# Hybrid encoder layer on one core: the last products in two banks, the final norms in another order, the first two tiles shared by ScalarE and DVE

## The chip, the cores and the metric

The kernel runs on one core of a Trainium2 chip. The metric is the device time of one execution in microseconds, taken as the median of several runs.

## The reference

One encoder layer in float32 on x of 512 positions and 1024 channels, and a final RMSNorm. Cut to what matters:

```python
def rms_norm(x, g):
    y = x * lax.rsqrt(jnp.mean(x * x, axis=-1, keepdims=True) + EPS)
    return y * g
...
h = rms_norm(x, attn_norm_g)
xr, gate, q, k, v = split(h @ w_in)          # 1024 -> 5 x 512
xr = centred_depthwise_conv(xr, conv_w, conv_b)
y_rnn = (rg_lru(xr, forward) + rg_lru(xr, backward)) * gelu(gate)
y_attn = dilated_attention(q, k, v, rel_bias)  # 8 heads, three dilated windows
mix = concat(rms_norm(y_rnn, norm_rnn_g), rms_norm(y_attn, norm_attn_g))
x = x + mix @ w_out                            # 1024 -> 1024
h = rms_norm(x, mlp_norm_g)
x = x + square(relu(h @ w_up)) @ w_down        # 1024 -> 4096 -> 1024
return rms_norm(x, final_norm_g)
```

## The kernel before

Every product of the projections is made of three matrix products in a reduced-precision float32 format ("fp32r"): each operand is split into a rounded part (hi) and the rest (lo = value - hi), and hi x hi, hi x lo and lo x hi are added in a PSUM bank. In the helper `mm3` these three are lines 303, 304 and 305. ScalarE mostly makes the hi part (a copy with rounding, line 251 for the weights), DVE the lo part (a subtraction, line 259). The order of the instructions on TensorE, ScalarE, DVE and GpSimd is the order in which the program writes them; only SP's queue of transfers is ordered by the framework.

**The start.** x comes transposed, in 8 tiles of 128 channels by 512 positions, each with 128 x 384 weights beside it (`xwt[k]`, lines 315 to 327). For each tile `cvx(k)` makes `h_hi` (x times the norm's gain, rounded, ScalarE, line 333), the weights' hi part (line 336 on DVE for tile 0, line 338 on ScalarE for the others), `h_lo` (line 339, DVE) and the weights' lo part `w3l` (line 340, DVE). `sq(k)` squares the tile on ScalarE, `addsq(k)` adds the squares into `sqx` on DVE (line 348). TensorE first runs 8 warm-up products (line 145). Then it works through the tiles in order, for three blocks of 128 output columns in three banks (`pxr`): tile 0 with the three blocks inside (line 412), the other tiles with `mm3` for one block after the other. Ahead of tile 7's products stands `col_sums(sqx)` (line 402), which sums the squares over the channels for the norm's factor; `rstd_cols` makes that factor on GpSimd. `softplus_consts` is a generator that makes eight-column constants for the recurrence on DVE, ScalarE and GpSimd in four portions; `next(spc)` issues a portion. Two are issued ahead of and behind tile 0, a third behind its square, the fourth much later.

**The middle** (input projection, recurrence, attention, output projection, and the MLP in two halves, with products of quadrants that share operands) is not touched.

**The end.** The down projection of the MLP's second half works through seven groups of products, of which "s4" is the last. It has two row tiles (`tt` 0 and 1), each with 4 x 2 steps of three products of 512 columns that are added onto a bank in which earlier groups stand already. The row tiles belong to positions 256 to 383 and 384 to 511, that is to the blocks 2 and 3 of the output; blocks 0 and 1 are complete after the group before. `x1n[g, n]` holds block g, column half n of the residual stream. `fin_half` squares a half and sums it over the row (ScalarE, line 1301). `fin(g)` adds the sums of both halves (line 1306), takes the root (line 1307, ScalarE) and the reciprocal (line 1308, DVE), multiplies the right half on ScalarE (line 1310; `xf` is that half times the gain already, line 1340) and issues its output from ScalarE's queue (line 1311), and multiplies the left half with factor and gain on DVE (line 1313) and issues it from SP's queue. `fin_other(g)` prepares the right half of block g. While the first row tile of "s4" runs, the norms of blocks 0 and 1 and `fin_other` of blocks 2 and 3 are issued; behind it come the addition `evac` (line 1488) and the norm of block 2, and behind the second row tile `fin_last`, which adds the product to the left half of the output (512 columns, worked on in two pieces of 256: lines 1319 and 1321), squares the pieces (lines 1320 and 1322), and makes root, reciprocal (1325, 1326) and outputs (1328 to 1333).

Of the kernel before, what the change touches and what calls it, by code (L numbers as in the profile page):

```python
# [14 lines left out]
AF = mybir.ActivationFunctionType  # L15
OP = mybir.AluOpType

P = 128
S = 512
D = 1024  # L20
# [13 lines left out]
HF = NF // 2  # L34
NQ = HF // 4
TH = S // 2

VEC = {}
_o = 0
# [60 lines left out]
def hybrid_kernel(ctx: ExitStack, tc, xw, xn, w_in, w_v, w_out, w_up, w_dn, gates, vecs, rel, onehot, fg, out):  # L100
    nc = tc.nc
# [28 lines left out]
    def vec(n, i):  # L130
        return vt[:, VEC[n] + i:VEC[n] + i + 1]
# [41 lines left out]
        yield cneg, chalf  # L173

    spc = softplus_consts()
    next(spc)


    chunks = []
# [122 lines left out]
    def mm3(o, a, b, first, last, on=False):  # L302
        nc.tensor.matmul(o, lhsT=a[0], rhs=b[0], start=bool(first), stop=False, skip_group_check=on)  # L303
        nc.tensor.matmul(o, lhsT=a[0], rhs=b[1], start=False, stop=False, skip_group_check=on)  # L304
        nc.tensor.matmul(o, lhsT=a[1], rhs=b[0], start=False, stop=bool(last), skip_group_check=on)  # L305
# [8 lines left out]
    h_hi = big.tile([P, KD, S], FR, name="h_hi", tag="bigA")  # L314
# [15 lines left out]

    def cvx(k):
        x, w = xwt[k][:, :S], xwt[k][:, S:]
        act(h_hi[:, k, :], x, AF.Copy, scale=vec("ag", k))
        hi, lo = g_("w3h", FR), g_("w3l", FR)
        if k == 0:
            nc.vector.tensor_copy(hi[:, :3 * P], w)
        else:
            act(hi[:, :3 * P], w, AF.Copy)
        stt(h_lo[:, k, :], x, vec("ag", k), f(h_hi)[:, k, :], op0=OP.mult, op1=OP.subtract)
        nc.vector.tensor_tensor(lo[:, :3 * P], w, f(hi)[:, :3 * P], op=OP.subtract)  # L340
        w3.append((hi, lo))

    def sq(k):
        sqx[k] = g_("sqx")
        act(sqx[k], xwt[k][:, :S], AF.Square)
# [2 lines left out]
        nc.vector.tensor_tensor(sqx[0], sqx[0], sqx.pop(k), op=OP.add)  # L348

    cvx(0)  # L350
    next(spc)
    sq(0)
    next(spc)
    for k in range(1, KD):
        cvx(k)
        sq(k)
        if k >= 2:
            addsq(k - 1)
# [532 lines left out]
    x1, x1n = {}, {}  # L891
# [237 lines left out]
    r2 = {}  # L1129
# [168 lines left out]
    def fin_half(tt, n):  # L1298
        s = small("sso", 1)
        scr = g_("scr")  # L1300
        act(scr, x1n[tt, n], AF.Square, accum_out=s)
        sso[tt, n] = s

    def fin(tt):
        r = small("rf", 1)
        nc.vector.tensor_tensor(r, sso[tt, 0], sso[tt, 1], op=OP.add)
        act(r, r, AF.Sqrt, scale=1.0 / D, bias=epsb)
        nc.vector.reciprocal(r, r)
        o = g_("ot")
        act(o, xf[tt], AF.Copy, scale=r)  # L1310
        nc.scalar.dma_start(out[tt * P:(tt + 1) * P, S:], o)
        o = g_("ot")
        stt(o, x1n[tt, 0], r, fgt[0], op0=OP.mult, op1=OP.mult)
        nc.sync.dma_start(out[tt * P:(tt + 1) * P, 0:S], o)

    def fin_last(tt, p):
        x, sa, sb, b = x1n[tt, 0], small("sso", 1), small("sso", 1), small("rf", 1)
        left, right = slice(0, TH), slice(TH, S)
        stt(x[:, left], p[:, left], r2[tt], x[:, left], op0=OP.mult, op1=OP.add)
        act(g_("scr")[:, left], x[:, left], AF.Square, accum_out=sa)  # L1320
        stt(x[:, right], p[:, right], r2[tt], x[:, right], op0=OP.mult, op1=OP.add)
        nc.vector.tensor_tensor_reduce(g_("scr")[:, right], x[:, right], x[:, right], 1.0, 0.0, OP.mult, OP.add, sb)
        act(b, sa, AF.Identity, scale=1.0 / D, bias=sso[tt, 1])
        r = small("rf", 1)
        act(r, sb, AF.Sqrt, scale=1.0 / D, bias=b)
        nc.vector.reciprocal(r, r)
        o = g_("ot")
        act(o, xf[tt], AF.Copy, scale=r)
        nc.scalar.dma_start(out[tt * P:(tt + 1) * P, S:], o)
        o = g_("ot")  # L1330
        for c in (left, right):
            stt(o[:, c], x[:, c], r, fgt[0][:, c], op0=OP.mult, op1=OP.mult)
            nc.sync.dma_start(out[tt * P:(tt + 1) * P, c], o[:, c])
# [23 lines left out]
    for half in range(2):  # L1357
# [132 lines left out]
        def evac(w, tt, p):  # L1490
            if w == "11":
                add(p, 0, tt, 0)
            elif w == "s1":
                add(p, 1, tt, 1)
            elif w == "s2":
                add(p, 0, tt, 1)
            elif w == "22":
                add(p, 0, tt, 1)
            elif w == "s3":
                add(p, 1, tt, 1)  # L1500
            elif w == "21":
                add(p, 0, tt, 0)
            else:
                add(p, 1, tt, 0)
                if half == 1:
                    fin_half(2 + tt, 0)
                    fin(2 + tt)

        def dmm(j, dst, tt, k2):
            _, w, q = seq[j]  # L1510
            hi, lo = splits[cd + j]
            sl = slice(k2 * S, (k2 + 1) * S)
            ah, al = opsplit[w, q]
            tsl = slice(k2 * TH + tt * P, k2 * TH + (tt + 1) * P)
            mm3(dst[tt], (ah[:, tsl], al[:, tsl]), (hi[:, sl], lo[:, sl]), q == 0 and k2 == 0 and w in ("11", "s1", "21"), q == NQ - 1 and k2 == 1, True)

        def dfeed(j, m):
            if m == 0:
                conv_hi(cd + j + 3)
            elif m == 1:  # L1520
                conv_lo(cd + j + 3)
            elif m == 2 and todo:
                a_hi(*todo[0])
            elif m == 3 and todo:
                a_lo(*todo.popleft())
# [36 lines left out]
                    nc.sync.dma_start(fgt[n], bass.AP(tensor=fg.tensor, offset=fg.offset + n * S, ap=[[0, P], [1, S]]))  # L1562
        if half == 1:
            b = 6 * NQ
            for tt in range(2):
                for j in range(b, b + NQ):
                    for k2 in range(2):
                        dmm(j, dst["s4"], tt, k2)
                        if tt == 0:
                            dfeed(j, 2 + k2)  # L1570
                    if tt == 0 and j == b:
                        conv_hi(cd + b + 3)
                        conv_lo(cd + b + 3)
                    if tt == 0 and j in (b + 1, b + 2):
                        fin_half(j - b - 1, 0)
                        fin(j - b - 1)
                    if tt == 0 and j == b + 3:
                        fin_other(2)
                        fin_other(3)
                if tt == 0:  # L1580
                    evac("s4", tt, dst["s4"][tt])
                else:
                    fin_last(3, dst["s4"][1])


# [54 lines left out]
```

## Time and profile before

| | |
|---|---|
| median of 3 runs | 543.67 us (543.66 to 544.35) |
| the profiled execution's own time | 544.4 us |
| its span, first to last instruction | 542.2 us |
| TensorE clock granted, mean | 0.997 |
| busy share: TensorE, weight loads, DVE, ScalarE, GpSimd | 98%, 84%, 80%, 67%, 12% |
| moved by DMA | 106.96 MB, mean 197 GB/s |

The profile is that of one execution. Times in its rows are microseconds from the span's start, and a row of the timeline gives start, length, engine, line, operation, output and inputs, and in brackets how long the engine was idle before it and what ended that. PE is TensorE's products, PEld its weight loads, which overlap the products; DVE is VectorE, ACT is ScalarE, POOL is GpSimd; SPq and ACTq are the queues that issue transfers. In rows of groups, the numbers behind the bar are the busy time in all in microseconds and the mean of one in nanoseconds.

### The profile page before, as it was taken

The numbers are of one execution on the slowest core, as the hardware profiler recorded it, in microseconds if no ns is written. First come the engines' busy times: TensorE is split into PE (matmuls) and PEld (weight loads), VectorE is DVE, ScalarE is ACT, GpSimd is POOL, SyncE is SP. The second block draws the span as 40 slices with busy tenths as digits, with TensorE's granted clock in tenths as the row PEclk, the third lists the DMA queues.
The fourth block names the chain that finished last, engine by engine and source line by source line (L and its number), as shares of the span: only waits on it lengthen the run. The fifth ranks groups of instructions, "written<-read, shape, count | busy, mean of one in ns | idle before, by whom it ended". The sixth has DMA issues, their size and how long they took to land.

```text
span 542.2 us, 8156 instructions
## 1 busy us (share of the span) xinstructions
PE 533.5 (98%) x3018; PEld 452.9 (84%) x3018; DVE 431.6 (80%) x628; ACT 363.4 (67%) x573; POOL 64.1 (12%) x91
## 2 busy tenths in 40 slices
PE   9999999999999999999999999999999999999994
PEld 7856888887887578889999888888999999888883
DVE  6897788996673599889769987879755888886984
ACT  7667983798774755677566855565645777755665
POOL 3330000000001031001030223001001020131000
PEclk9999999999999999999999999999999999999998
DMA  7754276454398788855676799994987397799704
GB/s 273 230 163 142 54 246 182 132 180 143 83 343 215 178 152 204 296 202 160 192 156 167 204 253 273 284 366 104 283 236 205 113 191 199 195 283 262 191 1 157
DMA packets 34360, 106.96 MB, mean 197 GB/s; under 512 B 4228, under 2 KB 5124, under 8 KB 34320
## 3 DMA queue, kind: packets, MB, share of 16 engines
q1 hardware_dynamic: 25600, 76.56, 41.4%
q0 software_dynamic: 7968, 28.76, 28.4%
q10 hardware_dynamic: 752, 1.12, 0.6%
q8 instruction: 24, 0.39, 0.3%
q14 instruction: 16, 0.13, 0.1%
HBM read 98.00 MB, written 4.23 MB: 189 GB/s over the span
## 4 chain that ended last, share of the span: by engine, by line
PE 87%; DVE 4%; ACT 4%; DMA 3%; issue 1%; ACTq 0%; DVEq 0%
PE pd L304 8%; PE pd L303 8%; PE pd L305 8%; PE pu L305 7%; PE pu L303 7%; PE pu L304 7%; PE pqk L303 3%; DMA tw<-in_w_up_dram 3%; PE pwo L303 3%; PE pqk L305 3%; PE pqk L304 3%; PE pav L859 3%; PE pt L778 3%; PE pwo L305 3%; PE pwo L304 3%; DVE wlo L259 2%
## 5 line engine op out<-in xcount | busy, mean ns | idle before, releaser
L259 DVE TENSOR_TENSOR wlo<-wraw,whi 128x1024 fp32r<-128x1024 f32 x73 | 89.0, 1221 | 21.4 <-ACT whi L251 21.1
L251 ACT ACTIVATE whi<-wraw 128x1024 fp32r<-128x1024 f32 x70 | 74.0, 1059 | 34.6 <-PE pd L305 19.5
L303 PE MATMUL pd<-whi,ah 128*128 128x512 f32 x192 | 74.7, 389 | 0.0
L304 PE MATMUL pd<-wlo,ah 128*128 128x512 f32 x192 | 74.7, 389 | 0.0
L305 PE MATMUL pd<-whi,al 128*128 128x512 f32 x192 | 74.7, 389 | 0.0
L251 ACT ACTIVATE whi<-tw 128x1024 fp32r<-128x1024 f32 x36 | 38.0, 1059 | 40.0 <-DMA tw<-in_w_up_dram 13.3
L304 PE MATMUL pu<-hl,whi 128*128 128x256 f32 x224 | 63.4, 283 | 0.0
L305 PE MATMUL pu<-hh,wlo 128*128 128x256 f32 x224 | 63.4, 283 | 0.0
L303 PE MATMUL pu<-hh,whi 128*128 128x256 f32 x224 | 63.4, 283 | 0.0
L305 PE MATMUL pu<-h2h,wlo 128*128 128x256 f32 (+1 forms) x200 | 60.1, 301 | 0.6 <-DVE wlo L259 0.6
L303 PE MATMUL pu<-h2h,whi 128*128 128x256 f32 (+1 forms) x200 | 60.1, 300 | 0.0
L304 PE MATMUL pu<-h2l,whi 128*128 128x256 f32 (+1 forms) x200 | 60.0, 300 | 0.0
L259 DVE TENSOR_TENSOR wlo<-tw,whi 128x1024 fp32r<-128x1024 f32 x36 | 44.0, 1223 | 19.5 <-ACT whi L251 19.5
L303 PEld LDWEIGHTS pu<-hh,whi 128*128 128x128 f32 x224 | 43.0, 192 | 0.0
L304 PEld LDWEIGHTS pu<-hl,whi 128*128 128x128 f32 x224 | 43.0, 192 | 0.0
L305 PEld LDWEIGHTS pu<-hh,wlo 128*128 128x128 f32 x224 | 43.0, 192 | 0.0
L251 ACT ACTIVATE whi<-ts 128x1024 fp32r<-128x1024 f32 x24 | 25.5, 1061 | 25.3 <-PE pd L305 18.3
L303 PEld LDWEIGHTS pd<-whi,ah 128*128 128x128 f32 x192 | 36.0, 188 | 7.5
L305 PEld LDWEIGHTS pd<-whi,al 128*128 128x128 f32 x192 | 36.0, 188 | 7.5
L304 PEld LDWEIGHTS pd<-wlo,ah 128*128 128x128 f32 x192 | 36.0, 188 | 7.4
L305 PEld LDWEIGHTS pu<-h2h,wlo 128*128 128x128 f32 x200 | 38.2, 191 | 2.1 <-DVE wlo L259 0.8
L304 PEld LDWEIGHTS pu<-h2l,whi 128*128 128x128 f32 x200 | 38.3, 191 | 1.3
(261 smaller groups left out, 1262.8 us busy)
## 6 DMA issues: line engine op xcount, KB each, us to landing
wraw<-in_w_up_dram SPq DMA_DIRECT2D x25, 512.0 KB, 4.1
ts<-in_w_dn_dram POOLq DMA_DIRECT2D x24, 512.0 KB, 13.9
wraw<-in_w_dn_dram SPq DMA_DIRECT2D x24, 512.0 KB, 9.2
tw<-in_w_up_dram SPq DMA_DIRECT2D x15, 512.0 KB, 9.9
tw<-in_w_up_dram POOLq DMA_DIRECT2D x15, 512.0 KB, 7.8
wraw<-in_w_in_dram SPq DMA_DIRECT2D x13, 512.0 KB, 3.5
ts<-in_w_dn_dram SPq DMA_DIRECT2D x8, 512.0 KB, 5.0
tw<-in_w_dn_dram SPq DMA_DIRECT2D x8, 512.0 KB, 8.0
```

The source lines that it names most:

```text
L251: act(hi, raws[i], AF.Copy)
L259: nc.vector.tensor_tensor(lo, r, f(splits[i][0]), op=OP.subtract)
L303: nc.tensor.matmul(o, lhsT=a[0], rhs=b[0], start=bool(first), stop=False, skip_group_check=on)
L304: nc.tensor.matmul(o, lhsT=a[0], rhs=b[1], start=False, stop=False, skip_group_check=on)
L305: nc.tensor.matmul(o, lhsT=a[1], rhs=b[0], start=False, stop=bool(last), skip_group_check=on)
L778: nc.tensor.transpose(pt[:, qt * P:(qt + 1) * P], en[h][qt][:, jt * P:(jt + 1) * P], ident)
L859: nc.tensor.matmul(pav[p][a, :], lhsT=vs[:, jt, h * DH:(h + 1) * DH], rhs=et.pop((h, jt)), start=jt == 0, stop=jt == 3)
```

## The change

Five edits, at the start and at the end of the kernel:

- Tiles 0 and 1: `h_hi` is made by ScalarE (256 columns of tile 0, 384 of tile 1) and by DVE (the other columns), and the weights' hi part by DVE for both tiles.
- Tile 1's products run like those of tile 0: hi x hi for the three blocks, then hi x lo, then lo x hi.
- The first three portions of the softplus constants are issued behind `cvx(1)`, `cvx(2)` and `cvx(3)`.
- The final norms are split into `fin_r` (sum and root) and `fin` and stand in another order: `fin_other(2)`, then block 0, block 1's root, `fin_other(3)`, and behind the first row tile block 2's square, block 1's outputs, block 2's root and outputs. All their outputs go through SP's queue.
- The last row tile's products: five of the eight steps with 512 columns as before, the last three (`NL`) for the left 256 columns into the same bank, and then for the right 256 columns into another bank (`pr`). `fin_left` adds the first bank (both halves, the right one without the last three steps) and squares the left piece while the right products run; `fin_right` adds the second bank, squares the right piece and makes the outputs. The gain is multiplied in ahead of the factor, so that the outputs are multiplications by a column: 512 columns on DVE, and of the other half 384 columns on ScalarE and 128 (`AC`) on DVE.

```diff
+NL = 3
+AC = 128
...
     spc = softplus_consts()
-    next(spc)
...
     def cvx(k):
         x, w = xwt[k][:, :S], xwt[k][:, S:]
-        act(h_hi[:, k, :], x, AF.Copy, scale=vec("ag", k))
         hi, lo = g_("w3h", FR), g_("w3l", FR)
-        if k == 0:
+        if k < 2:
+            c = (2 * P, 3 * P)[k]
+            act(h_hi[:, k, :c], x[:, :c], AF.Copy, scale=vec("ag", k))
+            nc.vector.tensor_scalar(h_hi[:, k, c:], x[:, c:], vec("ag", k), None, op0=OP.mult)
             nc.vector.tensor_copy(hi[:, :3 * P], w)
         else:
+            act(h_hi[:, k, :], x, AF.Copy, scale=vec("ag", k))
             act(hi[:, :3 * P], w, AF.Copy)
...
     cvx(0)
-    next(spc)
     sq(0)
-    next(spc)
     for k in range(1, KD):
         cvx(k)
+        if k < 4:
+            next(spc)
         sq(k)
...
-        if k == 0:
+        if k < 2:
             for i, (a, b) in enumerate(((0, 0), (0, 1), (1, 0))):
                 for t in range(3):
-                    nc.tensor.matmul(pxr[t], lhsT=wk(t, 0)[a], rhs=hk(0)[b], start=i == 0, stop=False)
+                    nc.tensor.matmul(pxr[t], lhsT=wk(t, k)[a], rhs=hk(k)[b], start=i == 0 and k == 0, stop=False)
             continue
...
-    def fin(tt):
-        r = small("rf", 1)
+    rfs = {}
+
+    def fin_r(tt):
+        r = rfs[tt] = small("rf", 1)
         nc.vector.tensor_tensor(r, sso[tt, 0], sso[tt, 1], op=OP.add)
         act(r, r, AF.Sqrt, scale=1.0 / D, bias=epsb)
+
+    def fin(tt):
+        r = rfs.pop(tt)
         nc.vector.reciprocal(r, r)
         o = g_("ot")
         act(o, xf[tt], AF.Copy, scale=r)
-        nc.scalar.dma_start(out[tt * P:(tt + 1) * P, S:], o)
+        nc.sync.dma_start(out[tt * P:(tt + 1) * P, S:], o)
...
+    def fin_left(tt, p):
+        x, sa, b = x1n[tt, 0], small("sso", 1), small("rf", 1)
+        xf[tt, 0] = g_("xf")
         stt(x[:, left], p[:, left], r2[tt], x[:, left], op0=OP.mult, op1=OP.add)
         act(g_("scr")[:, left], x[:, left], AF.Square, accum_out=sa)
         stt(x[:, right], p[:, right], r2[tt], x[:, right], op0=OP.mult, op1=OP.add)
+        nc.vector.tensor_tensor(xf[tt, 0][:, left], x[:, left], fgt[0][:, left], op=OP.mult)
+        act(b, sa, AF.Identity, scale=1.0 / D, bias=sso[tt, 1])
+        return b
+
+    def fin_right(tt, p, b):
+        x, sb, r = x1n[tt, 0], small("sso", 1), small("rf", 1)
+        stt(x[:, right], p[:, right], r2[tt], x[:, right], op0=OP.mult, op1=OP.add)
         nc.vector.tensor_tensor_reduce(g_("scr")[:, right], x[:, right], x[:, right], 1.0, 0.0, OP.mult, OP.add, sb)
         act(r, sb, AF.Sqrt, scale=1.0 / D, bias=b)
+        nc.vector.tensor_tensor(xf[tt, 0][:, right], x[:, right], fgt[0][:, right], op=OP.mult)
         nc.vector.reciprocal(r, r)
+        rows = out[tt * P:(tt + 1) * P, :]
+        o, o1 = g_("ot"), g_("ot")
+        act(o1[:, AC:], xf[tt][:, AC:], AF.Copy, scale=r)
+        nc.scalar.dma_start(rows[:, S + AC:], o1[:, AC:])
+        nc.vector.tensor_scalar(o, xf[tt, 0], r, None, op0=OP.mult)
+        nc.sync.dma_start(rows[:, :S], o)
+        nc.vector.tensor_scalar(o1[:, :AC], xf[tt][:, :AC], r, None, op0=OP.mult)
+        nc.sync.dma_start(rows[:, S:S + AC], o1[:, :AC])
...
+                if j == b:
+                    conv_hi(cd + b + 3)
+                    conv_lo(cd + b + 3)
+                    fin_other(2)
+                if j == b + 1:
+                    fin_half(0, 0)
+                    fin_r(0)
+                if j == b + 2:
+                    fin_half(1, 0)
+                    fin(0)
+                    fin_r(1)
+                    fin_other(3)
+            evac("s4", 0, dst["s4"][0])
+            fin_half(2, 0)
+            fin(1)
+            fin_r(2)
+            fin(2)
+            ks = [(j, k2) for j in range(b, b + NQ) for k2 in range(2)]
+            for j, k2 in ks[:-NL]:
+                dmm(j, dst["s4"], 1, k2)
+            for j, k2 in ks[-NL:]:
+                dmm(j, dst["s4"], 1, k2, left)
+            pr = ps_("pd", "pj")
+            for j, k2 in ks[-NL:]:
+                dmm(j, [None, pr], 1, k2, right, (j, k2) == ks[-NL])
+            bl = fin_left(3, dst["s4"][1])
+            fin_right(3, pr, bl)
```

More of the change, by code (lines that the diff above doesn't have):

```diff
@@ L1314, in fin @@
         nc.sync.dma_start(out[tt * P:(tt + 1) * P, 0:S], o)
-    def fin_last(tt, p):
-        x, sa, sb, b = x1n[tt, 0], small("sso", 1), small("sso", 1), small("rf", 1)
-        left, right = slice(0, TH), slice(TH, S)
+    def fin_left(tt, p):
+        x, sa, b = x1n[tt, 0], small("sso", 1), small("rf", 1)
+        xf[tt, 0] = g_("xf")
         stt(x[:, left], p[:, left], r2[tt], x[:, left], op0=OP.mult, op1=OP.add)
@@ L1504, in evac, with dmm @@
                 add(p, 1, tt, 0)
[L1505 to L1509, printed above, removed]
+        def dmm(j, dst, tt, k2, c=slice(0, S), new=False):
             _, w, q = seq[j]
             hi, lo = splits[cd + j]
-            sl = slice(k2 * S, (k2 + 1) * S)
+            sl = slice(k2 * S + c.start, k2 * S + c.stop)
             ah, al = opsplit[w, q]
             tsl = slice(k2 * TH + tt * P, k2 * TH + (tt + 1) * P)
-            mm3(dst[tt], (ah[:, tsl], al[:, tsl]), (hi[:, sl], lo[:, sl]), q == 0 and k2 == 0 and w in ("11", "s1", "21"), q == NQ - 1 and k2 == 1, True)
+            mm3(dst[tt][:, c], (ah[:, tsl], al[:, tsl]), (hi[:, sl], lo[:, sl]), new or q == 0 and k2 == 0 and w in ("11", "s1", "21"), q == NQ - 1 and k2 == 1, True)
         def dfeed(j, m):
@@ L1564, in hybrid_kernel @@
             b = 6 * NQ
[L1565 to L1583, printed above, removed]
+            for j in range(b, b + NQ):
+                for k2 in range(2):
+                    dmm(j, dst["s4"], 0, k2)
+                    dfeed(j, 2 + k2)
+                if j == b:
[25 more added lines that the diff above has]
+            fin_right(3, pr, bl)
 def kernel(**inputs):
```

9 lines of the change are left out of this document (removed).

## The prediction

> **What bounds the kernel now.** I read the page's first part, then its chain, then the chain again as a list in order of time, and last the instructions of the first 21 us and of the last 10 us, because the diff touches only these.
>
> ```profile
> span 542.2 us, 8156 instructions
> PE 533.5 (98%) x3018; PEld 452.9 (84%) x3018; DVE 431.6 (80%) x628; ACT 363.4 (67%) x573; POOL 64.1 (12%) x91
> PE 87%; DVE 4%; ACT 4%; DMA 3%; issue 1%; ACTq 0%; DVEq 0%
> ```
>
> TensorE is busy for 98% of the span and carries 87% of the chain. So time is won only where TensorE waits, or after its last product. The list of waits has one row of TensorE in the middle of the kernel:
>
> ```profile
> PE pu L305 <- DVE wlo L259: 0.6, 1, 0.6
> ```
>
> The change leaves that place alone. The start is in the chain in order of time (start, length, what):
>
> ```profile
> 1.04 3.79 PE pwarm L145 x16
> ...
> 7.79 0.37 PE pxr L303
> 8.16 0.38 PE pxr L304
> 8.54 0.46 PE pxr L305
> ```
>
> The last three are the first products of tile 1 of x; the first row is the warm-up, behind which tile 0 begins. A product that waits for nothing takes 0.227 us (at the end: 534.86 - 529.42 = 5.44 us for 24 of them, rows below). Three would take 0.68 us and took 0.37 + 0.38 + 0.46 = 1.21 us: 0.53 us are lost, because the three need in turn the rounded weights, the rest of x and the rest of the weights of this tile, one operation late each. The operations, by the timeline:
>
> ```profile
> 3.78 0.17 DVE L153 SCALAR_TENSOR_TENSOR e<-vt 128x8 f32<-128x8 f32 x1 [2.78 <-DMA vt<-in_vecs_dram]
> 3.86 0.17 DVE L154 TENSOR_SCALAR sp<-vt 128x8 f32<-128x8 f32 x1
> ...
> 5.67 0.17 DVE L158 TENSOR_SCALAR z<-e 128x8 f32<-128x8 f32 x1
> 5.87 0.20 DVE L159 RECIPROCAL z<-z 128x8 f32<-128x8 f32 x1
> 6.47 0.72 ACT L333 ACTIVATE h_hi<-tw,vt 128x512 fp32r<-128x512 f32 x1 [1.36 <-DMA tw<-in_xw_dram]
> 7.23 0.75 DVE L339 SCALAR_TENSOR_TENSOR h_lo<-tw,vt,h_hi 128x512 fp32r<-128x512 f32 x1 [1.16 <-ACT h_hi L333]
> 7.90 0.55 DVE L340 TENSOR_TENSOR w3l<-tw,w3h 128x384 fp32r<-128x384 f32 x1
> 8.78 0.75 DVE L339 SCALAR_TENSOR_TENSOR h_lo<-tw,vt,h_hi 128x512 fp32r<-128x512 f32 x1 [0.33 <-ACT h_hi L333]
> 17.47 0.74 DVE L339 SCALAR_TENSOR_TENSOR h_lo<-tw,vt,h_hi 128x512 fp32r<-128x512 f32 x1
> 18.60 1.47 DVE L348 TENSOR_TENSOR sqx<-sqx 128x512 f32<-128x512 f32 x2
> 20.22 0.41 PEld L402 LDWEIGHTS pcs<-ones,sqx 128*128 128x128 f32 x2
> ```
>
> The last row is the column sum of squares. It stands in TensorE's order ahead of tile 7 and loads sqx, the sum that DVE finishes at 18.60 + 1.47 = 20.07. Before, TensorE came 0.15 us after that sum was ready.
>
> The end, by the timeline:
>
> ```profile
> 529.42 0.39 PE L305 MATMUL pd<-whi,al 128*128 128x512 f32 x1
> 534.86 0.39 PE L305 MATMUL pd<-whi,al 128*128 128x512 f32 x1
> 534.90 0.75 DVE L1313 SCALAR_TENSOR_TENSOR ot<-x1n,rf,fgt 128x512 f32<-128x512 f32 x1
> 535.57 0.48 DVE L1319 SCALAR_TENSOR_TENSOR x1n<-pd,r,x1n 128x256 f32<-128x256 f32 x1
> 535.97 0.47 DVE L1321 SCALAR_TENSOR_TENSOR x1n<-pd,r,x1n 128x256 f32<-128x256 f32 x1
> 536.48 0.42 DVE L1322 CUSTOM_DVE_ANT_0 scr<-x1n 128x256 f32<-128x256 f32 x1
> 537.00 0.29 ACT L1325 ACTIVATE rf<-sso,rf 128x1 f32<-128x1 f32 x1
> 537.33 0.16 DVE L1326 RECIPROCAL rf<-rf 128x1 f32<-128x1 f32 x1 [0.42 <-ACT rf L1325]
> 537.53 0.88 DVE L1332 SCALAR_TENSOR_TENSOR ot<-x1n,rf,fgt 128x256 f32<-128x256 f32 x2
> 538.04 0.81 SPq L1333 DMA_DIRECT2D out_dram<-ot  x2
> 538.28 0.34 ACTq L1329 DMA_DIRECT2D out_dram<-ot  x1
> ```
>
> TensorE ends at 534.86 + 0.39 = 535.25. DVE is then still in the norm of the tile before (until 535.65), and from 535.57 to 537.53 five dependent steps follow, then the output.
>
> **The start, step by step.** Tile 0: DVE gets 256 columns of h_hi and loses the two softplus steps at 3.78. The warm-up ends at 1.04 + 3.79 = 4.83 in either kernel, and before, h_hi was there at 3.78 + 0.72 = 4.50 by the like row of tile 1; so I take zero, and 0.1 us either way. Tile 1: ScalarE's 384 columns instead of 512. The weights' 384 columns take ScalarE 508 ns and the full 0.72 us row has a scale besides, so I estimate 0.60 us, and h_hi ends at 7.07. DVE's 128 columns and its copy of the weights fit into the 1.16 us in which it idled: a copy of 512 columns takes 427 ns (row below), the two are less than that each, and both are bounded by 0.85 us together, about 0.2 us late at worst. The rest of x then starts at 7.11 instead of 7.23 and the weights' rest ends at 8.33. In the new order (three products with the rounded pair, three with the rest of x, three with the rest of the weights) these are wanted 0.68 and 1.36 us after TensorE's start at about 7.63, at 8.31 and 8.99; they are there at 7.86 and 8.33. So the whole 0.53 us is gone at tile 1.
>
> It does not come through to tile 7. DVE has nothing idle from 7.11 on: rest of x to rest of weights 0.67, to the next operation 0.47, the moved e and sp 0.17, so tile 2 starts at 8.42 instead of 8.78. Then five tiles at (17.47 - 8.78)/5 = 1.74 us each, and the moved z and reciprocal, 0.20 + 0.12: tile 7 at 17.43 instead of 17.47. The sum of squares ends at 20.03, TensorE is there at 20.22 - 0.53 = 19.69 and waits until about 20.08; behind it wait tile 7's nine products and the row norm that is made of this sum, and all of them move with it. Net gain 0.14 us, with 0.53 as the other end if the sum of squares didn't hold it, and zero if z costs more. The eight-column work of GpSimd moves behind z, from 6 to about 12 us; its next user there is the reciprocal root after 21 us.
>
> **The end, step by step.** Prices for what is new:
>
> ```profile
> 279.03 0.28 PE L304 MATMUL pu<-h2l,whi 128*128 128x256 f32 x1
> 279.15 0.28 PE L305 MATMUL pu<-h2h,wlo 128*128 128x256 f32 x1
> L434 DVE CAST ohr<-oht 97x512 fp32r<-97x512 f32 x2 | 0.9, 427 | 0.1
> L442 DVE TENSOR_SCALAR nbs<-pbias 8x512 f32<-8x512 f32 x2 | 1.3, 670 | 0.0
> L338 ACT ACTIVATE w3h<-tw 128x384 fp32r<-128x384 f32 x4 | 2.0, 508 | 0.0
> L1488 DVE SCALAR_TENSOR_TENSOR x1n<-pd,r,x1n 128x512 f32<-128x512 f32 x11 | 8.1, 745 | 0.0
> L1301 ACT ACTIVATE scr<-x1n 128x512 f32<-128x512 f32 x7 | 4.3, 621 | 0.9 <-ACT ot L1310 0.9
> L1310 ACT ACTIVATE ot<-xf,rf 128x512 f32<-128x512 f32 x3 | 2.2, 723 | 0.7 <-DVE rf L1308 0.7
> DMA to landing us min/median/max: 1.9/2.3/2.7
> ```
>
> TensorE: products of 256 columns follow each other by 0.12 us. The last 9 of 512 columns become 9 left and 9 right ones, 18 x 0.12 = 2.16 for 9 x 0.227 = 2.04 us: 0.12 us more. The first of these nine starts at 534.86 - 8 x 0.227 = 533.05, so the left ones end at 533.05 + 8 x 0.12 + 0.28 = 534.29, the right ones at 535.37.
>
> The reordered norms: the tile before ends on TensorE at 529.42 + 0.39 = 529.81. Behind it come its addition 0.75, its square 0.62 (+0.2 for the accumulator), tile 1's output on ScalarE 0.72, the root 0.29, the reciprocal 0.16 and its own output 0.75, together 3.5 us: about 533.4, because the two squares and the norm of tile 0 now stand ahead of 529.8. DVE is free 0.9 us before the left half arrives. The issues moved from ScalarE's queue to SP's (0.34 to 0.38 us each) have only outputs behind them there.
>
> Left half: addition at 534.32, the addition of the right half's first sums 0.40 later, the multiplication with the gain 0.40 later (256 columns, 0.42 as in L1322); DVE takes the next at 535.46. The right half's last addition goes there, 0.06 us after its products. Then as before: 0.51 to the square, 0.52 to the root, 0.33 to the reciprocal (the right multiplication lies under the root), 0.20: the outputs start at 537.02 instead of 537.53, 0.51 us earlier.
>
> Outputs: DVE multiplies 512 columns by a column. The trace has no such operation on SBUF: the bounds are 427 ns (copy, one source) and 670 ns (from PSUM) or the 0.75 of L1313. I take 427, the nearest row with one source in SBUF. SP's first issue is at 537.48 instead of 538.04, ScalarE's (384 columns, about 0.61) at 537.65 instead of 538.28, SP's second at 537.89 instead of 538.48 (538.85 less an issue of 0.37), and that one carries 64 KB instead of 128. The Trainium skill, VectorE: DVE Perf Modes, section on mode 2x_2P, says that an fp32 operation with one tensor source runs at two elements a cycle from SBUF and not from PSUM; by it the price is the copy's, by the PSUM row the sum would lose 0.24 us.
>
> The last issue landed after 1.9 to 2.7 us; the one that counted before is SP's second, 538.48 + 2.7 = 541.18, with 1.02 us from there to the span's end. After, 537.89 + 2.7 = 540.6 at worst and 539.8 at best; the same bytes follow each other, so I take 540.4. Gain at the end 0.78 us (0.58 to 1.38).
>
> **Sum.** 0.14 + 0.78 = 0.92 us. The profiled execution took 544.4 us, 2.2 us beside its span of 542.2; I expect 543.5 and 541.3 after. The median of the runs shown is 543.67, 0.7 below that execution, and two of the three runs lie there, so I take the change from there: 542.75, or 542.8 us, 0.17% less. 0.2%, or 1.09 us, is about what a measurement of this kernel can tell from no change: the forecast lies just inside.
>
> **Rivals.** (1) The sum of squares doesn't hold TensorE: 0.53 + 0.78 = 1.31 us, 542.4. Against it: the DVE rows from 8.78 to 17.47 leave no gap. Chance 0.12. (2) The outputs land nearer the best end: with 0.95 to 1.38 us at the end and 0.14 at the start the gain passes 1.09, 542.2 to 542.6. For it: less is in the last issue. Chance 0.27. (3) The column multiplication costs what L442 costs, or the last small transfer takes its 2.7 us, or both: 0.2 to 0.6 us, 543.1 to 543.5. Chance 0.09. The Trainium skill, DMA: Bandwidth & Descriptors, section Measured, calls transfers under 64 KB descriptor-dominated and gives 0.95 us for one of 64 KB; as an estimate that would be about half a microsecond more than I allow, and no row here shows one. (4) Slower: the second up-projection, where the chain leaves TensorE.
>
> ```profile
> 389.90 7.96 DMA tw<-in_w_up_dram
> ```
>
> There a load, ScalarE and DVE hand the time to TensorE with no slack (the 0.6 us wait above ends this stretch). If the shifted start makes this load meet others, each microsecond more is one of the kernel; from 0.9 us on the gain is gone, from 2.0 us on it is slower by over 0.2% (544.8). Nothing in the diff touches that order, and a shift of 0.14 us is small. Chance 0.07. That the edit does not do what it says is not in question: the halves are separate instructions.
>
> **Numbers.** Forecast 0.45, rivals 0.12, 0.27, 0.09, 0.07. Faster by over 0.2%: 0.12 + 0.27 = 0.39; within: 0.45 + 0.09 = 0.54; slower: 0.07. The range from 542.3 to 543.5 takes in the first, second and third and leaves out the slower case and the edges.
>
> **What would show it.** In the profile after: no gap between the products of tile 1; a wait of about 0.4 us at the column sum, released by DVE's sqx, and the load there at 20.1; the left addition at about 534.2, less than 0.1 us after its products; the outputs' multiplications half a microsecond earlier, the 512-column one at 0.43 us. A column sum at 19.7 would mean that I was wrong on DVE's chain; a multiplication of 0.67 us or a last landing beyond 540.6, on the outputs; an up-projection that ends later than the start's gain allows, on the rest.

## The result, and the profile after

| | before | after |
|---|---|---|
| median, first comparison (10 runs each) | 543.84 us | 542.23 us (541.85 to 542.65) |
| ratio, with its 95% interval | | 0.997 (0.9961 to 0.998) |
| the profiled execution, its span | 544.4 us, 542.2 us | 541.95 us, 540.0 us |

The change is faster by 1.6 us, with an interval of 1.1 to 2.1 us: faster by 0.3% (0.2 to 0.39%), where the forecast had 0.17%; the time lies 0.07 us below the forecast's range. In a later comparison (experiment 9) the same kernel had 542.13 us against 543.57.

The page's first part and its chain, of after:

```profile
span 540.0 us, 8180 instructions
PE 532.7 (99%) x3027; PEld 453.1 (84%) x3027; DVE 433.1 (80%) x634; ACT 362.8 (67%) x572; POOL 65.2 (12%) x91
PE 95%; DVE 2%; DMA 1%; issue 1%; ACT 0%; SPq 0%; DVEq 0%; ACTq 0%
```

TensorE has nine products more (18 halves for 9 whole ones) and carries 95% of the chain. Before it was 87%, because the chain left TensorE in the second up-projection. That wait is not in after's list; among the rows of TensorE's products the only new one is the one forecast, at the column sum (engine, line, what was waited for, then total, times, longest in us):

```profile
PE pcs L406 <- DVE sqx L352: 0.2, 1, 0.2
```

The start of after, by the timeline:

```profile
6.44 0.62 ACT L337 ACTIVATE h_hi<-tw,vt 128x384 fp32r<-128x384 f32 x1 [1.63 <-DMA tw<-in_xw_dram]
6.44 0.29 DVE L338 TENSOR_SCALAR h_hi<-tw,vt 128x128 fp32r<-128x128 f32 x1 [0.82 <-DMA tw<-in_xw_dram]
7.09 0.75 DVE L343 SCALAR_TENSOR_TENSOR h_lo<-tw,vt,h_hi 128x512 fp32r<-128x512 f32 x1
8.38 0.74 DVE L343 SCALAR_TENSOR_TENSOR h_lo<-tw,vt,h_hi 128x512 fp32r<-128x512 f32 x1
...
17.34 0.74 DVE L343 SCALAR_TENSOR_TENSOR h_lo<-tw,vt,h_hi 128x512 fp32r<-128x512 f32 x1
18.47 1.48 DVE L352 TENSOR_TENSOR sqx<-sqx 128x512 f32<-128x512 f32 x2
20.00 0.97 PEld L406 LDWEIGHTS pcs<-ones,sqx 128*128 128x128 f32 x8 [0.62 <-DVE sqx L352]
7.29 0.85 PE L416 MATMUL pxr<-h_hi,w3h 128*128 128x512 f32 x3
7.97 0.89 PE L416 MATMUL pxr<-h_lo,w3h 128*128 128x512 f32 x3
8.69 0.85 PE L416 MATMUL pxr<-h_hi,w3l 128*128 128x512 f32 x3
```

The products of tile 1 (the last three rows, three products each) begin 0.68 and 0.72 us apart, that is almost without a gap. DVE begins tile 2 at 8.38 and tile 7 at 17.34, and the column sum's load waits 0.62 us for the sum that ends at 18.47 + 1.48 = 19.95.

The end of after, by the timeline:

```profile
533.83 0.28 PE L306 MATMUL pd<-whi,al 128*128 128x256 f32 x1
531.25 0.75 DVE L1322 SCALAR_TENSOR_TENSOR ot<-x1n,rf,fgt 128x512 f32<-128x512 f32 x1
533.07 0.48 DVE L1330 SCALAR_TENSOR_TENSOR x1n<-pd,r,x1n 128x256 f32<-128x256 f32 x1 [1.07 <-PE pd L306]
533.47 0.47 DVE L1332 SCALAR_TENSOR_TENSOR x1n<-pd,r,x1n 128x256 f32<-128x256 f32 x1
533.86 0.41 DVE L1333 TENSOR_TENSOR xf<-x1n,fgt 128x256 f32<-128x256 f32 x1
534.20 0.47 DVE L1339 SCALAR_TENSOR_TENSOR x1n<-pd,r,x1n 128x256 f32<-128x256 f32 x1
535.76 0.48 DVE L1348 TENSOR_SCALAR ot<-xf,rf 128x512 f32<-128x512 f32 x1
536.16 0.28 DVE L1350 TENSOR_SCALAR ot<-xf,rf 128x128 f32<-128x128 f32 x1
536.40 0.37 ACTq L1347 DMA_DIRECT2D out_dram<-ot  x1
536.27 0.33 SPq L1349 DMA_DIRECT2D out_dram<-ot  x1
536.70 0.38 SPq L1351 DMA_DIRECT2D out_dram<-ot  x1
```

TensorE ends at 533.83 + 0.28 = 534.11. DVE is free 1.07 us before the left half is there, the right half's last addition starts 0.09 us behind the last product, and the outputs' multiplications start 1.65 us behind it; before it was 537.53 - 535.25 = 2.28. The last issues, by the page's part on DMA cut to that stretch (size in KB, then us from issue to landing):

```profile
out_dram<-ot SPq DMA_DIRECT2D x1, 256.0 KB, 2.0
out_dram<-ot ACTq DMA_DIRECT2D x1, 192.0 KB, 2.5
out_dram<-ot SPq DMA_DIRECT2D x1, 64.0 KB, 2.4
```

The last one lands at 536.70 + 2.38 = 539.08, which is 4.97 us behind TensorE's end. Before it landed at 538.48 + 2.74 = 541.22, 5.97 us behind it.

**Where the time came from.** Three marks of each profile, in us:

| kernel | tile 1 there | column sum's load | behind tile 1 | tile 7's first product, behind tile 1 | TensorE's end | last landing | behind TensorE's end |
|---|---|---|---|---|---|---|---|
| before | 6.47 | 20.22 | 13.75 | 14.78 | 535.25 | 541.22 | 5.97 |
| before again (4) | 6.60 | 20.30 | 13.70 | 14.73 | 534.82 | 540.82 | 6.00 |
| start only (1) | 6.14 | 19.70 | 13.56 | 14.48 | 533.85 | 539.82 | 5.97 |
| end only (2) | 6.85 | 20.58 | 13.73 | 14.76 | 534.97 | 539.95 | 4.97 |
| after | 6.44 | 20.00 | 13.56 | 14.48 | 534.11 | 539.08 | 4.97 |
| after again (9) | 6.56 | 20.12 | 13.56 | 14.47 | 534.31 | 539.28 | 4.97 |

"Tile 1 there" is the start of its h_hi on ScalarE, which waits for the transfer. It moves by 0.7 us between executions, and in these six the whole start moves with it; so the start has to be read from there, not from zero. Read so, the start edits bring the column sum's load forward by 0.17 us. The load understates it: in before it runs 0.22 us ahead of its product (20.22 and 20.44), in after TensorE stands idle and both begin at 20.00. The first product of tile 7, behind the column sum, comes 0.28 us earlier. Its rows in before and in after:

```profile
21.25 0.49 PE L303 MATMUL pxr<-h_hi,w3h 128*128 128x512 f32 x1
20.92 0.48 PE L304 MATMUL pxr<-h_hi,w3h 128*128 128x512 f32 x1
```

The end edits bring the last landing 1.00 us nearer to TensorE's end. Of that 0.12 us goes for the longer split products, so 0.88 us is left.

### The profile page after: what moved, and what is told of

Same layout as the page of the kernel before. It is cut to its first block, busy times and chain, and to the rows that moved or that the text cites. A ratio compares the mean times of both kernels' runs of the same rounds, so it can differ in the third digit from the quotient of the medians.

```text
span 540.0 us, 8180 instructions
## 1 busy us (share of the span) xinstructions
PE 532.7 (99%) x3027; PEld 453.1 (84%) x3027; DVE 433.1 (80%) x634; ACT 362.8 (67%) x572; POOL 65.2 (12%) x91
## 4 chain that ended last, share of the span: by engine, by line
PE 95%; DVE 2%; DMA 1%; issue 1%; ACT 0%; SPq 0%; DVEq 0%; ACTq 0%
PE pu L305 10%; PE pu L306 10%; PE pu L304 10%; PE pd L305 9%; PE pd L304 9%; PE pd L306 9%; PE pqk L304 3%; PE pwo L304 3%; PE pqk L306 3%; PE pqk L305 3%; PE pav L863 3%; PE pt L782 3%; PE pwo L306 3%; PE pwo L305 3%; PE pg L493 2%; PE pv L304 2%
## 5 line engine op out<-in xcount | busy, mean ns | idle before, releaser
L305 PE MATMUL pd<-wlo,ah 128*128 128x512 f32 (+1 forms) x195 | 75.2, 386 | 0.0
L304 PE MATMUL pd<-whi,ah 128*128 128x512 f32 (+1 forms) x195 | 75.2, 386 | 0.0
L306 PE MATMUL pd<-whi,al 128*128 128x512 f32 (+1 forms) x195 | 75.2, 386 | 0.0
L304 PEld LDWEIGHTS pu<-h2h,whi 128*128 128x128 f32 x200 | 38.3, 191 | 1.4 <-ACT hm L1088 0.2
```

## Experiments

**1 and 2: one half of the change each.** Before with the edits of `cvx`, the softplus portions and tile 1's order alone; and after with those taken back.

```diff
 (start only, against before)
-        act(h_hi[:, k, :], x, AF.Copy, scale=vec("ag", k))
-        if k == 0:
+        if k < 2:
+            c = (2 * P, 3 * P)[k]
+            act(h_hi[:, k, :c], x[:, :c], AF.Copy, scale=vec("ag", k))
+            nc.vector.tensor_scalar(h_hi[:, k, c:], x[:, c:], vec("ag", k), None, op0=OP.mult)
...
 (end only, against after: the same lines the other way)
```

> The kernel before with the change's edits at the start alone (shared rounding of tiles 0 and 1, tile 1's order, the softplus portions later); the end is the old one. Theory 1 (the parts add up, the column sum holds TensorE, and the missing stall in the second up-projection is chance): faster by 0.3 us, column sum's first load at about 20.0 us, a wait of up to 0.9 us in the up-projection in some profiles still. Theory 2 (the earlier start itself removes the stall in the up-projection): faster by 0.6 to 1.2 us, and no wait of TensorE after 400 us.

> The kernel before with the change's edits at the end alone; the start is the old one. Theory 1: faster by 1.0 us, last landing about 3.85 us behind the end of TensorE's last product instead of 5.97. Theory 2: faster by 1.0 us, and the profile shows the wait in the up-projection, since TensorE starts as late as before. If the end gave 1.3 us or more, both would be short at the end.

Measured beside before's 543.72 us: start only 543.50 (ratio 0.9991, 0.9983 to 1.0), end only 542.79 (0.9983, 0.9974 to 0.9992). That is 0.22 and 0.93 us, together 1.15. The median spans say the same: 541.6 before, 541.4 and 540.7. So most of the gain is the end's. The table shows that neither half reaches into the other: start only has before's 5.97 us at the end, end only has before's 13.73 us at the start. The last landing of end only was expected 3.85 us behind TensorE's end; it came after 4.97, as in after. End only starts late (tile 1 at 6.85) and still has no wait in the second up-projection, so that wait doesn't need an early start to go.

**3: the softplus portions out of the way.** After, with the three portions behind the column sum and the first two pieces of the convolution (`conv_a`).

```diff
         cvx(k)
-        if k < 4:
-            next(spc)
...
     conv_a(1, pxr[1])
+    for _ in range(3):
+        next(spc)
     cneg, chalf = next(spc)
```

> The changed kernel with the three softplus portions issued behind the column sum instead of behind tiles 1 to 3. Theory 1: DVE's chain to the sum of squares gets 0.17 + 0.32 us shorter, the column sum's load moves from 20.0 to about 19.5 us and the kernel gains 0.4 to 0.5 us over the changed one. Rival (the column sum is not what holds the start, or its later chain through GpSimd gives it back): the same time as the changed kernel within 0.1 us.

Measured: 543.09 us (0.999, 0.9981 to 0.9999), 0.9 us slower than after, which neither theory had. The sum of squares came 0.27 us earlier (landing + 13.24 instead of 13.51), but a wait behind it took more back than that, in the list of waits:

```profile
PEld pg L491 <- DVE xr L463: 1.4, 1, 1.4
```

The eight-column work on DVE now stood inside the convolution, and the gates' products waited for it. Most of it was no work: DVE waited 0.94 us for ScalarE's exponential, which stood behind ScalarE's part of the convolution.

```profile
27.84 0.17 DVE L160 TENSOR_SCALAR z<-e 128x8 f32<-128x8 f32 x1 [0.94 <-ACT e L158]
```

Whether the chain that the work was taken from was the right one, experiments 5 and 10 show.

**4: before again,** unchanged.

> The kernel before once more, for a second profile and the spread. Theory 1: a ratio of 1, and a wait in the up-projection that differs from the 0.8 us of the first profile. Theory 2: the wait is there again, 0.6 to 0.9 us.

Measured: 543.85 us (1.0, 0.9992 to 1.0009). Its profile lacks before's wait in the second up-projection and has another one, in the first, by the list of waits:

```profile
PEld pu L303 <- ACT hm L1084: 0.5, 1, 0.5
```

So a wait of the middle can stand in one execution of a kernel and be missing in the next.

**5 and 10: the softplus portions into DVE's idle time.** After, with the three portions behind tile 0, where DVE waits for tile 1 to land; run twice.

```diff
     cvx(0)
+    next(spc)
     sq(0)
+    next(spc)
+    next(spc)
     for k in range(1, KD):
         cvx(k)
-        if k < 4:
-            next(spc)
```

> The changed kernel, but its first three softplus portions stand behind tile 0's operations, where DVE idles until tile 1 of x lands, instead of behind cvx(1), cvx(2) and cvx(3). Theory A (the chain of DVE from the landing of tile 1 to the sum of squares sets the column sum): that chain loses the 0.17 + 0.17 + 0.17 + 0.20 us of the four eight-column operations and their gaps, 0.3 to 0.5 us; sum of squares at the landing + 13.1 instead of + 13.5, the wait at the column sum 0.3 instead of 0.7 us, the kernel 0.25 to 0.45 us faster than the changed one. Theory B (another load or ScalarE's work sets DVE's pace from tile 2 on): the sum of squares stays at the landing + 13.5 and the time stays. Theory C: ScalarE's exponential, ahead of tile 1 in ScalarE's order, waits for DVE and delays h_hi of tile 1; then the chain starts late by up to 0.3 us and the time stays or is worse.

> The changed kernel with the three softplus portions behind tile 0's operations, once more, beside the changed kernel. Theory A (the 1.6 us wait in the second up-projection of the first profile was a late transfer in that one execution): no such wait in this profile, the load that GpSimd issues at about 410 us lands after 5.1 to 5.5 us instead of 8.45, and the median is 0.15 to 0.35 us under that of the changed kernel. Theory B (the earlier start brings that load into collision): the load takes over 6.5 us again, TensorE waits 0.8 us or more there, and the time is the changed kernel's or worse.

Measured: 542.17 us in 6 runs (0.9968, 0.9955 to 0.998), and 541.88 us in 12 runs (0.9962, 0.995 to 0.9975) beside 542.13 of after in the same comparison. The first one's profile had the shorter chain (sum of squares at landing + 13.17) and then lost more than that in the second up-projection, by the timeline:

```profile
436.41 0.38 PE L306 MATMUL pu<-h2h,wlo 128*128 128x256 f32 x1 [1.60 <-DVE wlo L260]
```

In the same profile every later step of ScalarE and DVE for that operand is late too, and behind them is a load which GpSimd issues at 410.41. Its row in the part on DMA (size, then us from issue to landing) of this kernel, of after, and of before, whose wait at the same place was 0.6 us:

```profile
tw<-in_w_up_dram POOLq DMA_DIRECT2D x1, 512.0 KB, 8.4
```

```profile
tw<-in_w_up_dram POOLq DMA_DIRECT2D x1, 512.0 KB, 5.3
```

```profile
tw<-in_w_up_dram POOLq DMA_DIRECT2D x1, 512.0 KB, 6.9
```

It was not alone: the load that SP issues 2.2 us ahead of it took 4.6 us in this profile and 4.4 in before's, and 3.3 in after's. In the repetition GpSimd's load landed after 5.24 us and there was no wait there; nor, by the timeline, at the column sum's load:

```profile
6.26 0.62 ACT L337 ACTIVATE h_hi<-tw,vt 128x384 fp32r<-128x384 f32 x1 [0.27 <-DMA tw<-in_xw_dram]
19.54 1.08 PEld L407 LDWEIGHTS pcs<-ones,sqx 128*128 128x128 f32 x8
```

The profiles show that DVE's chain from the landing to the sum of squares sets the column sum: with 0.32 us less of it (13.19 for 13.51) TensorE came to the column sum without a wait, and tile 7's first product stood 14.32 us behind the landing, 0.16 us less than in after. The times agree with that and can't show it alone: the median is 0.25 us lower and the median span 0.3 us (539.95 against 540.25), inside the intervals. The 1.6 us wait goes with transfers that were late in one execution; that the earlier start brings it on is not shown, and the 12 runs of the repetition, of 541.28 to 542.68 us, have no sign of it.

**6, 7 and 8: the end without one of its parts.** After without the second bank (all products 512 columns wide, so that the additions, squares and gain multiplications all stand behind the last product); with the norms in the old order and their right halves issued from ScalarE's queue; with the last block's outputs made as before. Cut to what matters:

```diff
 (6)
-            for j, k2 in ks[:-NL]:
+            for j, k2 in ks:
                 dmm(j, dst["s4"], 1, k2)
...
-            fin_right(3, pr, bl)
+            fin_right(3, dst["s4"][1], bl)
 (7)
+                if j in (b + 1, b + 2):
+                    fin_half(j - b - 1, 0)
+                    fin_r(j - b - 1)
+                    fin(j - b - 1)
+                if j == b + 3:
                     fin_other(2)
...
                     fin_other(3)
 (8)
+        act(o1, xf[tt], AF.Copy, scale=r)
+        nc.scalar.dma_start(rows[:, S:], o1)
+        for c in (left, right):
+            stt(o[:, c], x[:, c], r, fgt[0][:, c], op0=OP.mult, op1=OP.mult)
+            nc.sync.dma_start(rows[:, c], o[:, c])
```

> The changed kernel, but the last row tile's products are all 512 columns wide in one bank; its additions, squares and gain multiplications therefore all stand behind the last product (the gain multiplication as one of 512 columns). Theory A (the split is what brings the end forward): TensorE ends 0.12 us earlier, but the left addition of 0.4 us and part of the gain's multiplication (0.75 - 0.42) come onto the path: 0.3 to 0.65 us slower than the changed kernel. Theory B (DVE is free early by the new order, and that alone brings the gain): at most 0.2 us slower.

> The changed kernel with the split and the column multiplications, but the final norms in the old order and with their right halves issued from ScalarE's queue. Theory A (split and order need each other): DVE is in block 2's output until about 0.9 us behind the point where the left half is complete, so the left addition starts late, the two left operations behind it push the right addition back, and 0.6 to 1.1 us of the end's 0.9 us gain are gone: about what the start alone gave. Theory B (the order is only tidiness, since DVE has 0.9 us between the left and right halves): less than 0.3 us slower.

> The changed kernel, but its last block's outputs are made as before: ScalarE multiplies all 512 columns of the right half, DVE makes the left half in two pieces of 256 with factor and gain together, and SP's last transfer carries 128 KB instead of 64. Theory A (the pieces are not what brings the gain): SP's second issue is at the same time, since it is held by SP's first issue of 0.33 us and not by DVE; the kernel is 0 to 0.15 us slower. Theory B (the smaller last transfer and ScalarE's shorter operation pay): 0.25 to 0.45 us slower, with a last landing after 2.7 instead of 2.4 us.

| kernel | median | ratio to before | median span | landing behind TensorE's end |
|---|---|---|---|---|
| after, first comparison | 542.23 | 0.997 (0.9961 to 0.998) | 540.35 | 4.97 |
| 6, no split | 542.67 | 0.9977 (0.9968 to 0.9986) | 540.7 | 5.41 |
| 7, old order | 544.26 | 1.0009 (0.9999 to 1.0018) | 542.4 | 7.06 |
| 8, no column multiplication | 542.69 | 0.9977 (0.9968 to 0.9986) | 540.6 | 5.03 |

No split: 5.41 less the 4.97 + 0.12 of after is 0.32 us, at the lower end of what was expected; the median lost 0.44.

Old order: 2.0 us slower, twice the expected. DVE, timeline of experiment 7, with its last product:

```profile
534.14 0.28 PE L306 MATMUL pd<-whi,al 128*128 128x256 f32 x1
533.97 0.75 DVE L1322 SCALAR_TENSOR_TENSOR ot<-x1n,rf,fgt 128x512 f32<-128x512 f32 x1
534.64 0.48 DVE L1330 SCALAR_TENSOR_TENSOR x1n<-pd,r,x1n 128x256 f32<-128x256 f32 x1
535.75 0.47 DVE L1339 SCALAR_TENSOR_TENSOR x1n<-pd,r,x1n 128x256 f32<-128x256 f32 x1
```

Block 2's output still holds DVE when the left half is complete; the left addition starts behind TensorE's end, and its three operations push the right half's addition to 1.33 us behind that end, where after has 0.09. That is 1.24 us, and the last transfer of 64 KB took 3.2 instead of 2.4 us for the other 0.83. Why it did, no row shows. It was hardly the chance of one execution, since the median span of this kernel's 11 runs (542.4) is 2.05 us above after's. With the old order the kernel with the split has an end 1.1 us longer than before's 5.97, while the kernel with the new order and without the split (5.41) still gains 0.56 of the 0.88 us: the order is what makes the split pay.

Column multiplication: the end is 0.06 us longer, as expected by the theory that it brings little. SP's second issue stands 0.94 us behind the start of the multiplications in both kernels (536.70 - 535.76, and 537.29 - 536.35). In both SP's first issue sets it: that one comes 0.51 us behind the start (536.27, and 536.86), and the second follows 0.43 us later; in after the small multiplication is done at 536.16 + 0.28 = 536.44, 0.26 us before its issue (in 8 the second piece is done at 537.23, 0.06 us before). The median lost 0.46 us, which that doesn't explain; 0.27 of it lies outside the span (below).

In this profile the start's gain is missing too: tile 7's first product stands 14.73 us behind the landing of tile 1, as in before. The rows of tile 2 in it, on ScalarE and on DVE:

```profile
8.08 0.73 ACT L341 ACTIVATE h_hi<-tw,vt 128x512 fp32r<-128x512 f32 x1 [0.28 <-DMA tw<-in_xw_dram]
8.84 0.75 DVE L343 SCALAR_TENSOR_TENSOR h_lo<-tw,vt,h_hi 128x512 fp32r<-128x512 f32 x1 [0.15 <-ACT h_hi L341]
```

Tile 2 came late, 1.42 us behind tile 1 (8.08 - 6.66), where ScalarE starts it 1.13 us behind in after, and DVE's chain stood still for it. In after this h_hi is ready 0.08 us before DVE begins tile 2, so the chain has about that much to spare; before's ScalarE came to tile 2 only 1.57 us behind tile 1 (8.04 - 6.47), so a tile 2 as late as this one would not have held it. The gain of the start hangs on a second transfer, which the prediction did not look at.

**9: after again,** beside experiments 10 and 11.

> The changed kernel once more, unaltered, for its scatter and as the reference of the two runs beside it. Theory A (the changed kernel's own steps give 0.30 us at the start and 0.88 at the end, and the rest of the 1.6 us first measured is the chance of the second up-projection's loads): the difference to the kernel before comes out between 1.0 and 1.5 us this time, and the profile shows the column sum at the landing of tile 1 + 13.56 and the last landing 4.97 us behind TensorE's last product. Theory B (the change also spares the stall in the second up-projection for good): 1.6 us or more again.

Measured: 542.13 us (0.9966, 0.9953 to 0.9978), with 13.56 and 4.97 us at the two ends, as in the first profile. By medians that is 1.44 us less than before, inside the first theory's 1.0 to 1.5; by the ratio it is 1.85 us, with an interval of 1.2 to 2.6, which holds the second's 1.6 too. The two are not told apart by the time.

**11: the column sum later.** After, with the column sum behind the first three of tile 7's products.

```diff
-        if k == KD - 1:
-            rcol = rstd_cols(col_sums(sqx[0], "et"), D)
...
             mm3(pxr[t], wk(t, k), hk(k), False, k == KD - 1)
+            if k == KD - 1 and t == 0:
+                rcol = rstd_cols(col_sums(sqx[0], "et"), D)
```

> The changed kernel, but the column sum of squares stands behind the first three of tile 7's nine products instead of ahead of them. Theory A (TensorE's 0.6 us wait at the column sum is the whole of what DVE's sum of squares costs): the wait goes, the products of tile 7 start 0.6 us earlier, and the kernel is 0.35 to 0.6 us faster than the changed one. Theory B (the sum of squares also holds what follows: column factors on GpSimd, 1.96 us, their transposition on TensorE, the row factor, the convolution and the gates): the wait turns up again at the transposition or at the gates' products, released by the factor or by DVE's xr, and the kernel gains less than 0.2 us or loses.

Measured: 542.06 us (0.9967, 0.9954 to 0.9979), 0.07 less than after. The wait went from the column sum and turned up again behind it, in the list of waits:

```profile
PEld prow L386 <- POOL rcol L394: 0.5, 1, 0.5
PEld pg L493 <- DVE xr L465: 0.5, 1, 0.5
```

TensorE waits for the factor that GpSimd makes of the sum, and then the gates' products wait for the convolution. The sum of squares holds the path, not only TensorE's place in the queue. How large these waits are is not to be compared with after: in this profile tile 2 was late again (ScalarE waited 0.51 us for it, DVE 0.37), and the sum of squares stood 13.98 us behind the landing of tile 1 instead of 13.51.

## Why the prediction was right in its steps and low in its sum

**The start.** The wait at tile 1 went, and the sum of squares took its place, as forecast: tile 2 at 8.38 (8.42 forecast), tile 7 at 17.34 (17.43), the load at 20.00 (20.08), after a wait of 0.62 us (about 0.4). The term was mis-sized: 0.14 us were forecast by the column sum's load, which moved by 0.17, while the first product behind it moved by 0.28. Tile 0, where nothing was forecast, also gained on TensorE: its last three products begin at 6.60 instead of 6.95. That time went into the wait at the column sum.

**The end.** Nearly every step came out at its number, counted from TensorE's end: left addition 1.04 us before it (1.05 forecast), outputs' multiplications 1.65 behind it (1.65), SP's issues at 2.16 and 2.59 (2.11 and 2.52), ScalarE's at 2.29 (2.28). The right half's last addition came 0.09 us behind its products; the prediction wrote 0.06 there, but its own figures (535.46 and 535.37) give 0.09. The column multiplication of 512 columns took 0.48 us, nearer to the copy's 427 ns than to the 670. From 128 to 512 columns it grew from 279 to 485 ns, 0.54 ns a column; an addition with two tensors grew from 475 (256 columns) to 745 ns, 1.05 ns a column, twice as much. The rule on two elements a cycle, which the prediction took from the Trainium skill (VectorE: DVE Perf Modes, section Mode 2×_2P), agrees with this trace. The last transfer took 2.38 us where 2.5 was allowed, and before's 2.74 where 2.7 was. Hence 0.88 instead of 0.78 us. The half a microsecond more for a transfer of 64 KB, which the prediction estimated from the Trainium skill (DMA: Bandwidth & Descriptors, section Measured), did not show in after; that section's row is of loads that GpSimd issues, while this transfer is a store from SP's queue. Experiment 7's 3.2 us is the one case like it.

**The sum.** 0.28 + 0.88 = 1.16 us instead of 0.92. This alone would have given 542.5, inside the range. The median span fell from 541.5 us in before's 89 later runs to 540.3 in after's 22, which fits the 1.16. The step that failed is the one from spans to times: "2.2 us beside its span of 542.2; I expect 543.5 and 541.3 after" held what lies outside the span constant and gave no reason for it. It isn't constant. Over before's runs beside the experiments and all recorded runs of the others:

| kernel | runs | time beside the span, median (range) |
|---|---|---|
| before | 89 | 2.13 us (2.07 to 2.25) |
| start only | 11 | 2.07 us (1.95 to 2.12) |
| end only | 11 | 2.04 us (1.89 to 2.09) |
| after | 22 | 1.92 us (1.85 to 2.03) |
| no column multiplication | 11 | 2.19 us (2.09 to 2.25) |

The 0.21 us between before and after are a gain that no row of a profile shows; where in the kernel it comes from stays open. With them the sum is 1.37 us, which from 543.67 gives 542.3, the edge of the range: the missing term of 0.21 and the terms mis-sized by 0.24 together moved the forecast there, and either alone would not have. The last 0.07 us are less than the scatter of after's runs (541.85 to 542.65). Before's median over its 89 runs is 543.70 and after's over 22 is 542.16, a difference of 1.54; the intervals of both comparisons take in 1.37. What is left, about 0.2 us, would fit the waits of the middle, which is not shown: 12 of 89 runs of before lay over 544.5, none of after's 22 over 542.65. Whether after is spared them for a reason or by chance stays open; one run of the kernel of experiment 5 was hit by the same wait.

**The rivals.** (1) The sum of squares does not hold TensorE: refuted by the wait in after, and by experiment 11, where it held the path behind as well. (2) Outputs nearer the best end: its time came (542.2, which it named and the range left out), its mechanism only by 0.1 us; that the two meet is luck. (3) A multiplication at 670 ns, or a last transfer of 2.7 us: neither in after. (4) The second up-projection: the place and the mechanism are real (a load that lands after 8.4 instead of 5.3 us, and 1.6 us of TensorE gone), but in the profiles it struck before and one later kernel, a repetition of the latter was free of it, and SP's load ahead was slow in the same executions; so no row ties it to the shift.

## What to carry to other kernels

Splitting the last products so that their evacuation starts early pays only when the engine that evacuates is already free: here the order of the norms was worth more than the split, and the split under the old order lost time. Small work on a busy in-order engine belongs into a gap where the engine waits for a transfer: the same eight-column operations held 0.3 us of a chain behind tiles 1 to 3, cost the kernel 0.9 us at the next tight place, where they waited for another engine, and no wait showed for them in the gap. Read a start from the landing of its data and an end from the last product, since in this kernel the landing alone moved by more than the edit was worth; and look which transfer comes next: the shortened chain here had 0.08 us to spare before tile 2 held it. When a forecast is made from spans, say what is assumed of the time outside them.

## What was not expected of the hardware

- The time that lies outside the profiled span differs between the kernels: 2.13 us before, 1.92 after, 2.19 without the column multiplications, each within some 0.2 us over all its runs; before's lowest (2.07) lies above after's highest (2.03). Its cause was not found.
- Tile 1's transfer was there between 6.06 and 7.04 us in the thirteen profiles, whatever the edits.
- The load that GpSimd issues at about 410 us landed after 5.1 to 5.4 us in ten profiles and after 6.7, 6.9 and 8.4 us in three; in two of these three TensorE's products waited for what is made of it. In the same three executions the load that SP issues just ahead took 4.4 to 4.6 us, in the other ten 3.1 to 3.3.
- ScalarE began tile 2 of x between 1.1 and 1.2 us behind tile 1 in eight of the ten profiles with the start edits, and 1.42 and 1.64 us behind in the other two, where it waited for tile 2's transfer.
